# Windowed attention in patches of 8 rows by 16 columns, normalised after the value product

## The chip, the core and the metric

The kernel runs on one core of a Trainium2 chip. Its engines work side by side, each through its own instructions in order: PE (TensorE, matmuls and transposes into PSUM), DVE (VectorE), ACT (ScalarE), POOL (GpSimd, which here works on SBUF alone) and SP, which issues the DMAs. They wait for each other by semaphores. The metric is the device time of one execution in microseconds (us).

## What is computed

One encoder block over 1024 tokens (a grid of 16 rows by 64 columns) of width 1024. The normed input is projected into several branches; three give attention-like outputs that are gated, merged and added to the input, and a mixture of 16 experts follows. The change is in the first and third branch. In the windowed one, a query sees the 8 rows by 16 columns of keys around it, clipped to the grid:

```
r_start = clip(r - 4, 0, 8)          # 8 rows of keys
col_start = clip(col - 8, 0, 48)     # 16 columns of keys
scores = q . k_win + rpb[:, row_off, col_off]
probs = softmax(scores over the 8*16 keys)
out = probs . v_win                  # 6 heads of 64
```

The memory branch is plain attention of the 1024 tokens to 256 memory rows (4 heads of 64). The second branch is a recurrence whose result goes through a group norm.

## The kernel before

All products are fp32 or, where three terms are summed (high x high, low x high, high x low part), in fp32r. The stages in order: projections; the recurrence, with the remaining 35 projection jobs (`fill_gen`) put between its steps on PE; the attention stage; the three branch products with gating; the output product with the router; the experts.

In the attention stage `items` lists 48 windowed items and 16 memory items, which go through a software pipeline: at step n, `PIPE` gives each part of an item and its lag, and the order in which the parts are written is the order of instructions on every engine. A windowed item before is one row of 64 queries for a pair j of heads: the queries of the two heads lie in the two halves of the 128 stationary columns (`qb`, zero in the other head's 64 partitions), and the 512 keys are 8 whole rows. Columns outside the window get -1e30 from the bias table. The parts are `score` (L221 to L223 into PSUM tile `s`, then bias, maximum on DVE, L862), `exp` (L867, ACT), `recip` and `mul` (L870, L873, DVE: the probabilities are divided by their sum), `trans` (four transposes, L878, into PSUM tile `tr`, copied to `pt` by ACT, L880), `mix` (value product into PSUM tile `av`, L887, one half of the columns of PE for each head), `hi` and `lo` (L891, L894: the result is split into `yh` and `yl` for the branch products).

`na_load(j)` fetches and splits keys and queries, and transposes values (`VT`) in 15 blocks of 128 positions. `group_norm` is a generator with nine stops for each of six blocks of 512 tokens; from step `GN0` on, one stop is taken in each step. `NB_` gives the number of PSUM buffers of each tile name. A DMA waits in SP's order.

Of the kernel before, what the change touches and what calls it, by code (L numbers as in the profile page):

```python
# [35 lines left out]
S = 1024  # L36
D = 1024
NM = 256
# [25 lines left out]
def shape_constants():  # L64
# [16 lines left out]
    w, k = p % 64, np.arange(64)  # L81
    st = np.clip(w - 8, 0, 48)
    ok = (k[None] >= st[:, None]) & (k[None] < st[:, None] + 16)
    c["nmask"] = np.where(ok, 0.0, NEG)
# [22 lines left out]
def lay(inputs):  # L107
# [14 lines left out]
    pad = np.pad(a["na_rpb"][0], ((0, 0), (0, 0), (48, 48)))  # L122
    st = pad.strides
    toe = np.lib.stride_tricks.as_strided(pad[:, :, 63:], (6, 64, 15, 64), (st[0], -st[2], st[1], st[2]))
    o["rpb"] = np.ascontiguousarray(toe.reshape(3, 128, 15, 64).transpose(1, 0, 2, 3).reshape(128, 3, 960))
# [18 lines left out]
    return {k: np.ascontiguousarray(v) for k, v in o.items()}  # L144


@with_exitstack
def block_kernel(ctx: ExitStack, tc: tile.TileContext, T, out, dbg=None, upto=99):
# [36 lines left out]
    pna = scratch("pna", (9, 128, S))  # L185
# [41 lines left out]
    pps = pre_ctx.enter_context(tc.tile_pool(name="pps", bufs=1, space=PSUM, reuse_waits="tile"))  # L227
    pctx = ExitStack()
# [430 lines left out]
    def fill_gen():  # L659
        jobs = []  # L660
        for j0, j1, fn, sc_, dst in ((11, 14, AF.Copy, 0.125, pna[0:3]), (14, 20, AF.Copy, 1.0, pna[3:9]),
                                     (20, 22, AF.Copy, 0.125, pmq), (22, 46, AF.Tanh, 0.5, pgt)):
            jobs += [(j, fn, sc_, dst[j - j0]) for j in range(j0, j1)]
# [88 lines left out]
    def abank(tag):  # L752
        return aps.tile([128, 512], F32, name=tag, bufs=NB_[tag])

# [60 lines left out]
    na = {}  # L815

    def na_load(j):
        bias = ap.tile([128, 15, 64], F32, name="bias", bufs=2)
        q = ap.tile([128, S], F32, name="q", bufs=2)
        kt = ap.tile([128, S], F32, name="kt", bufs=1)  # L820
        VC = ap.tile([128, S], F32, name="VC", bufs=1)
        for t, src in ((kt, pna[3 + j]), (q, pna[j]), (VC, pna[6 + j]), (bias.rearrange("p r c -> p (r c)"), T["rpb"][:, j])):
            SP.dma_start(t, src)
        VT = ap.tile([128, 15, 128], F32, name="VT", bufs=2)
        qb = [ap.tile([128, 16, 2, 64], F32R, name=f"qb{v}", bufs=2) for v in "hl"]
        KT = [ap.tile([128, S], F32R, name=f"KT{v}", bufs=2) for v in "hl"]
        na[j] = bias, KT, qb, VT
        yield
        for v in (slice(0, 512), slice(512, 1024)):
            A.activation(KT[0][:, v], kt[:, v], AF.Copy)  # L830
            G.tensor_tensor(KT[1][:, v], kt[:, v], KT[0][:, v].bitcast(F32), op=OP.subtract)
            yield
        q = q.rearrange("p (r t) -> p r t", t=64)
        for h, r in ((0, 0), (1, 0), (0, 8), (1, 8)):
            hi, lo = (v[:, r:r + 8, h] for v in qb)
            V.tensor_scalar(hi, q[:, r:r + 8], C("hsel")[:, h:h + 1], None, op0=OP.mult)
            yield
            V.scalar_tensor_tensor(lo, q[:, r:r + 8], C("hsel")[:, h:h + 1], hi.bitcast(F32), op0=OP.mult, op1=OP.subtract)
            if r:
                yield  # L840
        G.tensor_tensor(bias, bias, C("nmask")[:, None, :].to_broadcast([128, 15, 64]), op=OP.add)
        for i0 in range(0, 15, 4):
            p = abank("tr")
            n = min(4, 15 - i0)
            for i in range(i0, i0 + n):
                t0 = i * 128 if i < 8 else (i - 8) * 128 + 64
                PE.transpose(p[:, (i - i0) * 128:(i - i0 + 1) * 128], VC[:, t0:t0 + 128], ident)
            A.activation(VT[:, i0:i0 + n], p[:, :n * 128].rearrange("p (i c) -> p i c", i=n), AF.Copy)
            yield

    def na_item(j, r):
        bias, KT, qb, VT = na[j]
        rs = min(max(r - 4, 0), 8)
        ro = rs - r + 7
        o = {}

        def score():
            s = abank("s")
            mm3(s, 0, 1, *(v[:, r].rearrange("p h t -> p (h t)") for v in qb), *(v[:, rs * 64:rs * 64 + 512] for v in KT))
            o["sb"] = sb = ap.tile([128, 512], F32, name="sb", bufs=4)  # L860
            o["st"] = st = ap.tile([128, 8], F32, name="st", bufs=4)
            V.tensor_tensor_reduce(out=sb, in0=s, in1=bias[:, ro:ro + 8, :].rearrange("p r c -> p (r c)"),  # L862
                                   scale=1.0, scalar=-3.0e38, op0=OP.add, op1=OP.max, accum_out=st[:, 0:1])
            V.tensor_scalar(st[:, 1:2], st[:, 0:1], -1.0, None, op0=OP.mult)

        def exp():
            A.activation(o["sb"], o["sb"], AF.Exp, bias=o["st"][:, 1:2], scale=1.0, accum_out=o["st"][:, 2:3])  # L867

        def recip():
            V.reciprocal(o["st"][:, 3:4], o["st"][:, 2:3])  # L870

        def mul():
            V.tensor_scalar(o["sb"], o["sb"], o["st"][:, 3:4], None, op0=OP.mult)  # L873

        def trans():
            p = abank("tr")
            for k in range(4):
                PE.transpose(p[:, k * 128:(k + 1) * 128], o["sb"][:, k * 128:(k + 1) * 128], ident)  # L878
            o["pt"] = ap.tile([128, 512], F32, name="pt", bufs=3)
            A.activation(o["pt"], p, AF.Copy)  # L880

        def mix():
            o["av"] = av = abank("av")
            for k in range(4):
                vi = (rs // 2 + k) if rs % 2 == 0 else 8 + (rs - 1) // 2 + k
                for h, q in enumerate((LO, UP)):
                    PE.matmul(av[q, 0:64], VT[:, vi, 64 * h:64 * h + 64], o["pt"][:, k * 128 + 64 * h:k * 128 + 64 * h + 64],  # L887
                              start=(k == 0), stop=(k == 3))

        def hi():  # L890
            A.activation(yh[:, j, r * 64:(r + 1) * 64], o["av"][:, 0:64], AF.Copy)  # L891

        def lo():
            V.tensor_sub(yl[:, j, r * 64:(r + 1) * 64], o["av"][:, 0:64], yh[:, j, r * 64:(r + 1) * 64].bitcast(F32))  # L894
# [3 lines left out]
    kv = ap.tile([128, 4, NM], F32, name="kv")  # L898
    kb = [ap.tile([128, 2, 2, NM], F32R, name=f"kb{v}") for v in "hl"]
    vm = ap.tile([128, 2, 256], F32, name="vm")  # L900
    qm = []

    def mem_load():
        SP.dma_start(kv, pkv.rearrange("j p t -> p j t"))
# [545 lines left out]
```

## Time and profile before

| | us |
|---|---|
| median of 3 runs (2363.93 to 2367.25) | 2364.92 |
| the profiled execution | 2365.14 |
| its span, first to last instruction | 2363.3 |
| PE busy in the span | 2251.8 (95%) |
| DVE busy | 1710.3 (72%) |
| ACT busy | 1338.9 (57%) |
| attention: first score to first branch product | 838.09 to 999.38 = 161.3 |

The execution lies 1.8 us above its span and 0.2 us above the median. PE's busy time counts each matmul to its modelled end, so neighbours overlap; what a stream of matmuls costs is read from the distance of their starts.

### The profile page before, as it was taken

What the parts mean: (1) busy time and instruction counts of PE and PEld (TensorE: products, weight loads), DVE (VectorE), ACT (ScalarE), POOL (GpSimd) and SP (SyncE); (2) the same over time, 40 slices, a digit from 0 to 9 for tenths busy, and PEclk for the clock granted to TensorE, in tenths of its full rate; (3) what the DMA queues carried; (4) which work ended last, traced back from release to release, by engine and by line L of the source; (5) the groups of instructions that cost most, each with busy time, mean ns of one, the idle gap of its engine ahead of it and who ended that gap; (6) DMA issues with size and microseconds to landing.
All of it is one profiled execution on the core that took longest, in us unless ns stands there. A gap on an engine that the chain in (4) does not pass through costs nothing.

```text
span 2363.3 us, 34407 instructions
## 1 busy us (share of the span) xinstructions
PE 2251.8 (95%) x12931; PEld 1825.8 (77%) x12931; DVE 1710.3 (72%) x2140; ACT 1338.9 (57%) x1631; POOL 602.7 (26%) x1187
## 2 busy tenths in 40 slices
PE   7999999999999989999938999999999999999996
PEld 6677787877778867777837888888888888888885
DVE  6556566556656278763276888888888988898887
ACT  5554233333333367721226777777777777777775
POOL 1000567666656334242040000000000000000001
PEclk9999999999999999999978999999999999999998
DMA  6335434443443252165396999999999999999995
GB/s 238 152 143 209 124 106 117 128 112 108 126 118 88 71 172 79 58 215 170 125 346 251 380 381 378 391 387 389 393 381 382 377 389 384 390 387 391 383 346 193
DMA packets 193911, 588.56 MB, mean 249 GB/s; under 512 B 53072, under 2 KB 97360, under 8 KB 144592
## 3 DMA queue, kind: packets, MB, share of 16 engines
q1 hardware_dynamic: 187120, 562.88, 64.6%
q0 software_dynamic: 4752, 17.30, 2.7%
q10 hardware_dynamic: 1872, 6.17, 0.7%
q8 instruction: 102, 1.67, 0.3%
q14 instruction: 65, 0.53, 0.1%
HBM read 517.56 MB, written 68.73 MB: 248 GB/s over the span
## 4 chain that ended last, share of the span: by engine, by line
PE 80%; DVE 11%; DMA 2%; POOL 2%; ACT 2%; issue 2%; SPq 0%; POOLq 0%; ACTq 0%; DVEq 0%
PE y L1317 14%; PE acc L695 12%; PE g L1305 5%; PE g L1306 5%; PE g L1308 5%; PE u L1305 5%; PE u L1306 5%; PE u L1308 5%; PE acc L221 3%; PE acc L222 3%; PE acc L223 3%; PE tr L1365 1%; DVE Gst L640 1%; PE av L887 1%; DVE rsl L218 1%
## 5 line engine op out<-in xcount | busy, mean ns | idle before, releaser
L1282 DVE TENSOR_TENSOR ewl<-raw,ewh 128x2048 fp32r<-128x2048 f32 x380 | 849.8, 2284 | 6.0 <-ACT ewh L1277 6.0
L1277 ACT ACTIVATE ewh<-raw 128x2048 fp32r<-128x2048 f32 x380 | 720.9, 1915 | 113.3 <-PE u L1306 84.4
L1324 POOL DMA_INDIRECT acc<-ye,idx x15 | 43.4, 2893 | 949.7 <-DVE ye L1323 872.2
L695 PE MATMUL acc<-hlo,wh 128*128 128x512 f32 x560 | 225.2, 402 | 0.0
L695 PE MATMUL acc<-hhi,wh 128*128 128x512 f32 x560 | 225.0, 402 | 0.0
L695 PE MATMUL acc<-hhi,wl 128*128 128x512 f32 x560 | 224.9, 402 | 0.0
L551 POOL TENSOR_TENSOR tmul<-tinv,blk 96x60 f32<-96x60 f32 (+24 forms) x496 | 174.3, 351 | 151.3 <-DMA blk<-ldr 113.7
L1305 PE MATMUL g<-ewh,xh 128*128 128x512 f32 x512 | 206.5, 403 | 0.0
L1305 PE MATMUL u<-ewh,xh 128*128 128x512 f32 x512 | 202.3, 395 | 0.0
L1306 PE MATMUL g<-ewh,xl 128*128 128x512 f32 x512 | 200.7, 392 | 0.0
L1306 PE MATMUL u<-ewh,xl 128*128 128x512 f32 x512 | 199.6, 390 | 0.0
L553 POOL TENSOR_TENSOR tinv<-tinv,tmul 96x60 f32<-96x60 f32 (+24 forms) x496 | 175.0, 353 | 38.9
L1317 PE MATMUL y<-ewh,ah 128*128 128x512 f32 x512 | 138.2, 392 | 0.7 <-ACT ah L217 0.7
L1317 PE MATMUL y<-ewl,ah 128*128 128x512 f32 x512 | 137.8, 391 | 0.0
L1317 PE MATMUL y<-ewh,al 128*128 128x512 f32 x512 | 137.7, 391 | 0.0
L1308 PE MATMUL g<-ewl,xh 128*128 128x512 f32 x512 | 137.4, 390 | 0.0
L1308 PE MATMUL u<-ewl,xh 128*128 128x512 f32 x512 | 137.1, 390 | 0.0
L218 DVE TENSOR_TENSOR wl<-wraw,wh 128x1024 fp32r<-128x1024 f32 (+1 forms) x60 | 76.0, 1268 | 66.0 <-ACT wh L217 66.0
L695 PEld LDWEIGHTS acc<-hlo,wh 128*128 128x128 f32 x560 | 106.0, 189 | 20.5
L695 PEld LDWEIGHTS acc<-hhi,wh 128*128 128x128 f32 x560 | 105.9, 189 | 20.1
L695 PEld LDWEIGHTS acc<-hhi,wl 128*128 128x128 f32 x560 | 105.9, 189 | 20.1
L217 ACT ACTIVATE ah<-tr 128x512 fp32r<-128x512 f32 x64 | 38.3, 598 | 143.6 <-PE tr L1365 143.6
(311 smaller groups left out, 4471.9 us busy)
## 6 DMA issues: line engine op xcount, KB each, us to landing
raw<-in_wg_dram SPq DMA_DIRECT2D x128, 1024.0 KB
raw<-in_wu_dram SPq DMA_DIRECT2D x128, 1024.0 KB
raw<-in_wd_dram SPq DMA_DIRECT2D x128, 1024.0 KB
wraw<-in_wt_dram SPq DMA_DIRECT2D x46, 512.0 KB
pt<-pz SPq DMA_DIRECT2D x16, 768.0 KB
pgt<-po SPq DMA_DIRECT2D x48, 256.0 KB
gt<-pgt SPq DMA_DIRECT2D x16, 768.0 KB
blk<-ldr SPq DMA_DIRECT2D x64, 96.0 KB
```

Source lines behind the costliest of these rows:

```text
L218: V.tensor_sub(lo, src, hi.bitcast(F32))
L221: PE.matmul(out_, lh, rh, start=(k_ == 0), stop=False)
L222: PE.matmul(out_, ll, rh, start=False, stop=False)
L551: G.tensor_tensor(tm[:, 0:m, 0:n], tt[:, 0:m, j:j + 1].to_broadcast([4 * NB, m, n]), lt[:, j, None, j + 1:32].to_broadcast([4 * NB, m, n]) ...
L553: G.tensor_tensor(tt[:, 0:m, j + 1:32], tt[:, 0:m, j + 1:32], tm[:, 0:m, 0:n], op=OP.add)
L695: PE.matmul(p, l[:, k], r[:, k, s0:s0 + 512], start=(k == 0 and i == 0), stop=(k == KD - 1 and i == 2))
L1277: A.activation(hi, raws[seq[n]], AF.Copy)
L1282: V.tensor_sub(lo, raws.pop(seq[n]), his[seq[n]].bitcast(F32))
L1305: PE.matmul(p, xh[:, 4 * b + k], wh[:, k], start=(b == 0 and k == 0), stop=False)
L1306: PE.matmul(p, xl[:, 4 * b + k], wh[:, k], start=False, stop=False)
L1308: PE.matmul(p, xh[:, 4 * b + k], wl[:, k], start=False, stop=(b == 1 and k == 3))
L1317: PE.matmul(py[n], l[:, 2 * b + k], r[:, k, n * 512:(n + 1) * 512], start=(f == 0 and b == 0 and i == 0 and k == 0), stop=(f == 3 and b == ...
```

## The change

A windowed item becomes a patch of 8 rows by 16 columns, 128 queries, for a pair of heads: 24 items in place of 48. Its keys are the 12 rows by 24 or 32 columns that hold every window of the patch, 288 or 384 keys for each head. Each head's score product uses only its 64 partitions of queries and keys, as a stationary of 64 rows, and the two heads write two banks of `s`. The bias table is laid out on the host for each kind of patch and carries the mask; it is fetched in six parts of 960 KB in place of three of 480 KB. The memory items get the same form. `mul` is gone: the value product runs on unnormalised probabilities, two more matmuls write the reciprocals, spread over 64 columns, beside it in `av`, ACT copies them to `rb`, and DVE multiplies (`out`). `yl` moves to POOL, half of the `pt` copies (all of the memory items') to DVE. `s` now takes four banks, so `gn` and `av` have one buffer each in place of two.

The projection jobs of the values store four overlapping column groups (`pvc`, 896 KB for a pair of heads in place of 512 KB), four copies and four DMAs for each half job in place of one; the keys of the first pair of heads are split straight from PSUM and never stored. The query split no longer masks. `group_norm` takes two stops in a step, from step 2 on.

```diff
@@ -51,11 +51,11 @@
-GN0 = 5
+GN0 = 2
...
-PIPE = (("hi", 6), ("exp", 1), ("recip", 2), ("lo", 6), ("mul", 2), ("score", 0), ("trans", 3), ("mix", 5))
-NB_ = dict(s=2, tr=2, gn=2, av=2)
+PIPE = (("out", 4), ("exp", 1), ("recip", 2), ("trans", 2), ("mix", 3), ("score", 0))
+NB_ = dict(s=2, tr=2, gn=1, av=1)
@@ -144,6 +137,26 @@
+NROW, NCOL, COL0S, CTYPE = 12, (24, 32, 24), (0, 8, 24, 40), (0, 1, 1, 2)
+BOFF = [0, 288, 672, 960]
+WSUM = sum(NCOL[t] for t in CTYPE)
@@ -679,6 +696,20 @@
                 _, fn, sc_, dst = jobs[n]
+                if n == 3:
+                    split_to(*(t[:, s0:s0 + 512] for t in kt0), p)
+                    continue
+                if 6 <= n < 9:
+                    at = 0
+                    for cg in range(4):
+                        w = NCOL[CTYPE[cg]]
+                        if cg % 2 == 0:
+                            po, a0 = pp.tile([128, 512], F32, name="po", bufs=2), 0
+                        A.activation(po[:, a0:a0 + 8 * w].rearrange("p (r c) -> p r c", c=w),
+                                     p.rearrange("p (r c) -> p r c", c=64)[:, :, COL0S[cg]:COL0S[cg] + w], AF.Copy)
+                        SP.dma_start(pvc[n - 6][:, at + s0 // 64 * w:at + (s0 // 64 + 8) * w], po[:, a0:a0 + 8 * w])
+                        at, a0 = at + 16 * w, 8 * w
+                    continue
@@ -750,7 +781,7 @@
     def abank(tag):
-        return aps.tile([128, 512], F32, name=tag, bufs=NB_[tag])
+        return aps.tile([128, 2, 512] if tag == "s" else [128, 512], F32, name=tag, bufs=NB_[tag])
@@ -812,173 +843,210 @@
+    def bias_load(m):
+        if m < 6:
+            bias[m] = ap.tile([128, 2, BOFF[3]], F32, name="bias", bufs=3)
+            SP.dma_start(bias[m], T["rpb"][m // 2, m % 2])
...
         def exp():
-            A.activation(o["sb"], o["sb"], AF.Exp, bias=o["st"][:, 1:2], scale=1.0, accum_out=o["st"][:, 2:3])
+            for h in range(2):
+                A.activation(o["sb"][h], o["e"][h], AF.Exp, bias=o["st"][:, 2 + h:3 + h], scale=1.0, accum_out=o["st"][:, 4 + h:5 + h])
...
-        def mul():
-            V.tensor_scalar(o["sb"], o["sb"], o["st"][:, 3:4], None, op0=OP.mult)
...
         def mix():
             o["av"] = av = abank("av")
-            for k in range(4):
-                vi = (rs // 2 + k) if rs % 2 == 0 else 8 + (rs - 1) // 2 + k
+            mix_of(o, av)
+            for h, q in enumerate((LO, UP)):
+                PE.matmul(av[q, 128:256], o["st"][:, 6 + h:7 + h].to_broadcast([128, 64]), ident, start=True, stop=True)
+            o["rb"] = rb = ap.tile([128, 128], F32, name="rb", bufs=2)
+            A.activation(rb, av[:, 128:256], AF.Copy)
+
+        def out():
+            y = ap.tile([128, 128], F32, name="y", bufs=3)
+            V.tensor_mul(y, o["av"][:, 0:128], o["rb"])
+            y = tokens(y)
+            A.activation(tokens(yh), y, AF.Copy)
+            G.tensor_tensor(tokens(yl), y, tokens(yh).bitcast(F32), op=OP.subtract)
...
+    def na_item(j, g):
+        rh, cg = g // 4, g % 4
...
+        def score(o):
+            KT, qb = na[j][:2]
+            s, st = abank("s"), o["st"]
+            for i, (a, b) in enumerate(((0, 0), (1, 0), (0, 1))):
                 for h, q in enumerate((LO, UP)):
...
+                    PE.matmul(s[:, h, :n], qb[a][q, rh, cg], grid(KT[b][q])[:, r0:r0 + NROW, c0:c0 + w], start=(i == 0), stop=(i == 2))
...
+            for h in range(2):
+                V.tensor_tensor_reduce(out=sb[:, h, :n], in0=s[:, h, :n], in1=bias[2 * j + rh][:, h, b0:b0 + n],
+                                       scale=1.0, scalar=-3.0e38, op0=OP.add, op1=OP.max, accum_out=st[:, h:h + 1])
+            V.tensor_scalar(st[:, 2:4], st[:, 0:2], -1.0, None, op0=OP.mult)
+
+        def trans(o):
+            o["pt"] = pt = ap.tile([128, 2, 384], F32, name="pt", bufs=3)
+            for h in range(2):
+                p = abank("tr")
+                for k in range(3):
+                    PE.transpose(p[:m, k * 128:(k + 1) * 128], o["sb"][h][:, k * m:(k + 1) * m], ident)
+                if h:
+                    V.tensor_copy(pt[:m, h], p[:m, :384])
+                else:
+                    A.activation(pt[:m, h], p[:m, :384], AF.Copy)
+
+        def mix(o, av):
+            for k in range(3):
+                for h, q in enumerate((LO, UP)):
+                    PE.matmul(av[q, 0:128], na[j][2][:m, cg, rh + k, 64 * h:64 * h + 64], o["pt"][:m, h, k * 128:(k + 1) * 128],
+                              start=(k == 0), stop=(k == 2))
...
     with tc.manual_schedule():
...
-        items = [(na_item, j, r) for j in range(3) for r in range(16)] + [(mem_item, j, i) for j in range(2) for i in range(8)]
-        side = {1: na_load(1), 17: na_load(2), 33: mem_load()}
+        items = [(na_item, j, g) for j in range(3) for g in range(8)] + [(mem_item, j, i) for j in range(2) for i in range(8)]
+        side = {0: na_load(1), 8: na_load(2), 16: mem_load()}
...
-            live.pop(n - 6, None)
+            live.pop(n - 4, None)
+            if n in (3, 7, 11):
+                bias_load(n // 4 + 3)
             extra = [g for g in extra if next(g, 0) is None]
             if n >= GN0:
+                next(gn, 0)
                 next(gn, 0)
```

On PE, in the steady part of the windowed items, one item stood before as follows (`s` scores, `tr` transposes, `av` the value product; a number behind x counts the same instruction in a row):

```order
L221 MATMUL s<-KTh,qbh 128x512
L222 MATMUL s<-KTh,qbl 128x512
L223 MATMUL s<-KTl,qbh 128x512
L878 MATMUL tr<-cst,sb 128x128 x4
L887 MATMUL av<-pt,VT 64x64 x8
```

Now one item, with a stop of the group norm behind its scores (`gn`), stands so:

```order
L963 MATMUL tr<-cst,sb 128x128 x6
L972 MATMUL av<-pt,VT 64x128 x6
L920 MATMUL av<-cst,st 64x128 x2
L950 MATMUL s<-KTh,qbh 128x288 x2
L950 MATMUL s<-KTh,qbl 128x288 x2
L950 MATMUL s<-KTl,qbh 128x288 x2
L816 MATMUL gn<-y_9140,cst 128x512
```

The transposes of the item two steps back and the value product of the one three steps back now stand between one item's scores and the next's. On DVE, in the same part, the order before was:

```order
L870 RECIPROCAL st<-st 128x1
L894 TENSOR_TENSOR yl<-av,yh 128x64
L873 TENSOR_SCALAR sb<-sb,st 128x512
L862 ISA sb,st<-s,bias 128x512
L862 ISA st 128x1
L864 TENSOR_SCALAR st<-st 128x1
```

Now it is (L926 is the multiplication that reads `av` and frees its one buffer; L965 the copy of the second head's transposes):

```order
L954 ISA sb,st<-s,bias 128x384
L954 ISA st 128x1
L954 ISA sb,st<-s,bias 128x384
L954 ISA st 128x1
L956 TENSOR_SCALAR st<-st 128x2
L833 TENSOR_TENSOR y_8858<-y_8858,gn 128x512
L926 TENSOR_TENSOR y<-av,rb 128x128
L911 RECIPROCAL st<-st 128x2
L965 COPY pt<-tr 96x384
```

The read of `av` stands behind the two bias passes of the item before, and behind the group norm's work (L833). On ACT, at the start of the stage, the order before was as follows (`KTh` the keys of the second pair of heads, `lg` the group norm's gate, which its tanh makes):

```order
L880 ACTIVATE pt<-tr 128x512
L891 ACTIVATE yh<-av 128x64
L867 ACTIVATE sb,st<-sb,st 128x512
L880 ACTIVATE pt<-tr 128x512
L780 ACTIVATE lg<-lg 128x1024
L891 ACTIVATE yh<-av 128x64
L867 ACTIVATE sb,st<-sb,st 128x512
```

Now it begins so (L908 the exponentials of an item's two heads):

```order
L908 ACTIVATE sb,st<-sb,st 128x384 x2
L967 ACTIVATE pt<-tr 96x384
L876 ACTIVATE KTh<-kt 128x512
L811 ACTIVATE lg<-lg 128x1024
L908 ACTIVATE sb,st<-sb,st 128x384 x2
```

The keys' first copy and `lg` now stand ahead of the third item's exponentials; before, `lg` stood behind the exponentials of six items of half the size.

## Rows read from the trace of the kernel before

**Rows 1.** Busy time by stretch: start and end, length, engines, PEclk, DMA, GB/s

```profile
core 0: us, PE busy (x) PEld busy (x) DVE busy (x) ACT busy (x) POOL busy (x), PEclk, DMA share, GB/s
...
838.10:858.00 19.90, 14.27 (x119) 9.41 (x117) 19.25 (x49) 11.99 (x30) 7.77 (x6) 1.00 0.63 221
858.00:955.00 97.00, 93.50 (x984) 71.63 (x984) 80.34 (x262) 74.90 (x194) 42.10 (x29) 0.98 0.24 82
955.00:991.60 36.60, 35.44 (x310) 25.61 (x308) 31.82 (x97) 30.18 (x99) 9.33 (x7) 1.00 0.09 30
```

**Rows 2.** Instructions in order of time on PE, one windowed item: start, length

```profile
933.67 0.50 PE L221 MATMUL s<-KTh,qbh 128*128 128x512 f32 x1
934.00 0.39 PE L222 MATMUL s<-KTh,qbl 128*128 128x512 f32 x1
934.24 0.39 PE L223 MATMUL s<-KTl,qbh 128*128 128x512 f32 x1
934.47 0.60 PE L878 MATMUL tr<-cst,sb 128*128 128x128 f32 x4
934.99 0.69 PE L887 MATMUL av<-pt,VT 128*64 128x64 f32 x16
935.61 0.50 PE L221 MATMUL s<-KTh,qbh 128*128 128x512 f32 x1
```

**Rows 3.** The same on PE, one memory item's value product

```profile
994.13 0.66 PE L963 MATMUL av<-pt,vm 128*64 128x128 f32 x8
994.73 0.65 PE L955 MATMUL tr<-cst,sb 128*128 128x128 f32 x4
```

**Rows 4.** The same on DVE: bias pass, its accumulator, negation, group norm

```profile
937.84 0.68 DVE L862 CUSTOM_DVE_ANT_0 sb<-s,bias 128x512 f32<-128x512 f32 x1
938.45 0.08 DVE L862 DVE_READ_ACCUMULATOR2_ANT st<- 128x1 f32 x1
938.56 0.15 DVE L864 TENSOR_SCALAR st<-st 128x1 f32<-128x1 f32 x1
938.63 0.68 DVE L802 TENSOR_TENSOR y<-y,gn 128x512 f32<-128x512 f32 x1
```

**Rows 5.** Groups of instructions, 838 to 1000: count, busy us, mean ns, idle before

```profile
L873 DVE TENSOR_SCALAR sb<-sb,st 128x512 f32<-128x512 f32 x48 | 35.9, 748 | 0.1
L867 ACT ACTIVATE sb<-sb,st 128x512 f32<-128x512 f32 x48 | 34.7, 723 | 17.0 <-DVE st L864 16.5 <-DVE st L870 0.4
...
L941 ACT ACTIVATE sb<-s,st 128x256 f32<-128x256 f32 x32 | 14.9, 474 | 4.0 <-DVE st L936 3.8
...
L935 DVE TENSOR_REDUCE st<-s 128x2 f32<-128x512 f32 x16 | 10.9, 682 | 0.0
...
L805 POOL TENSOR_TENSOR y<-y,b 128x512 f32<-128x512 f32 x6 | 8.1, 1345 | 33.8 <-ACT yh L891 26.9 <-ACT y L804 6.9
...
L970 DVE TENSOR_TENSOR yl<-av,yh 128x128 fp32r<-128x128 f32 x16 | 4.6, 285 | 3.1 <-ACT yh L967 2.9
...
L786 ACT ACTIVATE y<-gn 128x512 f32<-128x512 f32 x6 | 3.6, 599 | 2.0 <-PE gn L785 2.0
L787 ACT ACTIVATE b<-gn 128x512 f32<-128x512 f32 x6 | 3.6, 595 | 0.0
```

**Rows 6.** The start of the stage: SP's issue, POOL's wait, traffic

```profile
839.68 0.44 SPq L759 DMA_DIRECT2D lg<-plat  x1
...
847.75 1.28 POOL L777 TENSOR_TENSOR y<-y,y 128x512 f32<-128x512 f32 x1 [0.94 <-DMA y<-yrw]
...
844.00:846.00 2.00, 1.32 (x8) 0.81 (x7) 1.93 (x6) 1.71 (x5) 1.10 (x2) 1.00 1.00 328
```

**Rows 7.** A stall on the second pair's keys, and PE's granted clock behind it

```profile
885.83 0.63 ACT L830 ACTIVATE KTh<-kt 128x512 fp32r<-128x512 f32 x1 [2.43 <-DMA kt<-pna]
...
888.23 1.09 PE L878 MATMUL tr<-cst,sb 128*128 128x128 f32 x4 [1.77 <-DVE sb L873]
...
889.00:890.00 1.00, 1.00 (x16) 0.75 (x16) 1.00 (x3) 1.00 (x3) 1.00 (x2) 0.50 0.10 39
```

More of the change, by code (lines that the diff above doesn't have):

```diff
@@ L144, in lay, with window_bias @@
     return {k: np.ascontiguousarray(v) for k, v in o.items()}
+NROW, NCOL, COL0S, CTYPE = 12, (24, 32, 24), (0, 8, 24, 40), (0, 1, 1, 2)
+BOFF = [0, 288, 672, 960]
+WSUM = sum(NCOL[t] for t in CTYPE)
+def window_bias(rpb, rh, ct):
+    cg = (0, 1, 3)[ct]
+    r, c = 8 * rh + np.arange(8), 16 * cg + np.arange(16)
+    kr, kc = 4 * rh + np.arange(NROW), COL0S[cg] + np.arange(NCOL[ct])
+    r0, c0 = np.clip(r - 4, 0, 8), np.clip(c - 8, 0, 48)
+    rows, cols = (kr[None] >= r0[:, None]) & (kr[None] < r0[:, None] + 8), (kc[None] >= c0[:, None]) & (kc[None] < c0[:, None] + 16)
+    inside = rows[:, None, :, None] & cols[None, :, None, :]
+    ir = np.clip(kr[None] - r[:, None] + 7, 0, 14)
+    ic = np.clip(kc[None] - c[:, None] + 15, 0, 30)
+    t = rpb[:, ir[:, None, :, None], ic[None, :, None, :]]
+    out = np.full(t.shape, NEG, np.float32)
+    out[:, inside] = t[:, inside]
+    return out.reshape(3, 2, 128, -1).transpose(0, 2, 1, 3)
 @with_exitstack
@@ new lines, in na_load @@
+        VC = ap.tile([128, 16 * WSUM], F32, name="VC", bufs=1)
+        qb = [ap.tile([128, 2, 4, 128], F32R, name=f"qb{v}", bufs=2) for v in "hl"]
+        KT = kt0 if j == 0 else [(ap if j == 1 else nq).tile([128, S], F32R, name=f"KT{v}") for v in "hl"]
+        na[j] = [KT, qb]
+        for rh in range(2):
+            SP.dma_start(q[:, 512 * rh:512 * rh + 512], pna[j][:, 512 * rh:512 * rh + 512])
+            if j == 0 and rh == 0:
+                bias_load(0)
+        if j:
+            kt = ap.tile([128, S], F32, name="kt", bufs=1)
+            SP.dma_start(kt, pna[3 + j])
@@ L851, in na_item @@
[L851 to L854, printed above, removed]
+        for rh in range(2):
+            hi, lo = (v[:, rh].rearrange("p g (r c) -> p g r c", c=16) for v in qb)
+            src = q[:, 512 * rh:512 * rh + 512].rearrange("p (r g c) -> p g r c", r=8, g=4)
+            A.activation(hi, src, AF.Copy)
+            (G if j else V).tensor_tensor(lo, src, hi.bitcast(F32), op=OP.subtract)
+            yield
+        VT = ap.tile([128, 4, 4, 128], F32, name="VT", bufs=2)
@@ new lines, in na_load, with attention @@
+        na[j].append(VT)
+        for cg in range(4):
+            p = abank("tr")
+            w = NCOL[CTYPE[cg]]
+            for i in range(4):
+                PE.transpose(p[:4 * w, i * 128:(i + 1) * 128], VW[cg][:, 4 * i * w:4 * (i + 1) * w], ident)
+            src, dst = p[:4 * w].rearrange("p (i c) -> p i c", i=4), VT[:4 * w, cg]
+            if cg % 2:
+                V.tensor_copy(dst, src)
+                yield
+            else:
+                A.activation(dst, src, AF.Copy)
+    def attention(score_of, trans_of, mix_of, tokens):
@@ L896, in na_item @@
-        return locals()
[L898 to L901, printed above, removed]
+            mix_of(o, av)
[3 more added lines that the diff above has]
+            A.activation(rb, av[:, 128:256], AF.Copy)
@@ L939, in exp, with tokens @@
-        def exp():
-            for h in range(2):
-                A.activation(o["sb"][:, h], o["s"][:, h * 256:(h + 1) * 256], AF.Exp, bias=o["st"][:, 2 + h:3 + h], scale=1.0,
-                             accum_out=o["st"][:, 4 + h:5 + h])
-        def recip():
-            V.reciprocal(o["st"][:, 6:8], o["st"][:, 4:6])
-        def mul():
-            for h in range(2):
-                V.tensor_scalar(o["sb"][:, h], o["sb"][:, h], o["st"][:, 6 + h:7 + h], None, op0=OP.mult)
-        def trans():
+        def tokens(y):
+            return y if y.ndim == 2 else y[:, 6 + j, ts]
@@ new lines, in score @@
+        def score(o):
+            s, st = abank("s"), o["st"]
+            for i_, (a, b) in enumerate(((0, 0), (1, 0), (0, 1))):
+                for h, q in enumerate((LO, UP)):
+                    PE.matmul(s[:, h, :NM], qm[j][a][q, ts], kb[b][q, j], start=(i_ == 0), stop=(i_ == 2))
+            V.tensor_reduce(st[:, 0:2], s[:, :, :NM], axis=AX.X, op=OP.max)
+            V.tensor_scalar(st[:, 2:4], st[:, 0:2], -1.0, None, op0=OP.mult)
+            sb = ap.tile([128, 2, 384], F32, name="sb", bufs=4)
+            o["e"], o["sb"] = ([t[:, h, :NM] for h in range(2)] for t in (s, sb))
```

162 lines of the change are left out of this document (69 added, 93 removed).

## Prediction

> **What bounds the kernel now.** The change touches the attention stage, so I read the busy time by stretch there first [rows 1]. From 858 to 955 PE is busy 93.5 of 97.0 us while DVE has 80.3: PE is the bound. In the first 20 us it is DVE, 19.25 of 19.90, with PE at 14.27. From 955 on the memory items run, PE again in front (35.4 of 36.6). Then I read one windowed item on PE in order of time [rows 2]: 1.94 us from one score to the next, 0.80 for three score products (starts some 0.24 apart), 0.52 for four transposes, 0.62 for the value product. Its sixteen records are eight pairs, the heads side by side: 0.46 at 0.058 a pair, with 0.16 left. 48 × 1.94 = 93 us and 36.6 for the memory items [rows 1]; the remaining 32 of the 161.3 us (table above) are the slow start, the group norm and the two ends. So the stage is bound by throughput: queues are deep enough that PE seldom waits.
>
> **The change, part by part.**
>
> *Work.* DVE loses the normalisation, 48 × 748 ns = 35.9 us [rows 5], and PE's score products have two thirds of the columns, for twice the queries. If throughput stayed the limit, this would be a large gain. But there is only one `av` buffer, and the order on PE and DVE shown above ties them into one ring for each item: PE's value product (L972) waits until DVE's L926 has read the item before; L926 stands on DVE behind the two bias passes, which need the scores that PE issued last; and the next scores stand on PE behind that value product. No other work of either engine shortens the ring; the transposes lie under DVE's part. So I price an item by the ring:
>
> - From the last score's start to DVE: a score runs 0.39 with 0.235 to the next start [rows 2], so 0.16 of drain, with a hand-over about 0.25.
> - Bias passes: 0.61 from start to start for 512 columns [rows 4]; between L970 (285 ns at 128 columns, [rows 5]) and L802 (0.68 at 512, [rows 4]) a column costs 1.03 ns, so a mean of 336 columns (half the patches have 288, half 384) takes 0.43. Each has an accumulator read of 0.11, and the negation 0.07 follows: 2 × 0.54 + 0.07 = 1.15.
> - L926, 128 columns from PSUM: 0.29 as L970, with hand-over 0.34.
> - Value product and reciprocals: 12 + 4 records, eight pairs of 128 columns at 0.11 (twice 0.058), and 0.16 for the change of form: 1.03. The memory product of before agrees, four pairs in 0.60 [rows 3].
> - Scores: 336/512 × 0.235 = 0.154 each. If the two heads' products, on the two halves of PE's rows, run together: 3 × 0.154 = 0.46; if one after the other, 0.92. No row has products on half the rows. The nearest is the value product, whose two halves of the columns do run together [rows 2], so I take 0.46 and keep 0.92 as a rival.
>
> Sum 3.2 us, × 24 = 77. [...]
>
> *Memory items.* The same ring with one reduction (682 ns, [rows 5]) in place of the two passes: 0.25 + 0.78 + 0.34 + six pairs 0.82 + scores of 256 columns 0.35 = 2.5, × 16 = 40 (before 36).
>
> ACT has two exponentials (474 ns at 256, 723 at 512 columns, [rows 5], so about 0.55 each), a copy of 0.45, and two small passes of 0.3: 2.2 an item, below 3.2, and it is off the ring. POOL has `yl`, 0.3 to 0.6, likewise covered. If that cover went, 2.2 would not bind until the ring fell below it.
>
> *Group norm.* Two stops in a step, with one `gn` buffer. Its twelve multiplications on DVE (0.61 each, L802, [rows 4]) stand inside the ring: 7.3 us. In three of the six blocks the centring product and the statistics fall into one step; PE then waits until ACT has copied and squared the first from the one buffer, 2 × 0.60 [rows 5], with the product of 0.24 to 0.6, ACT's own queue and two hand-overs about 2.4: 7. In the other three, POOL's addition (1345 ns, [rows 5]) and the multiplication behind it share a step, about 0.6 each on DVE: 2. Together 17. Before, PE was the bound and DVE's share was hidden. From below: only the 7.3, if ACT is early; from above: 25, if all six blocks wait 2.4.
>
> *Start.* Before the first score may start, `VC` (896 KB) and a bias part come ahead: 1.5 us. Then ACT's copy of the second pair's keys and the tanh of `lg` stand ahead of the third item's exponentials, and the group norm starts three steps earlier. Traffic is full there, 328 GB/s [rows 6]; before, POOL's first addition, behind 5760 KB, could start at 847.75 [rows 6]. By the diff 7936 KB now come ahead, 2176 KB or 6.6 us more, so near 854. On PE the first centring product, which needs it, stands behind the fourth item's scores, three periods of 3.2 after a first score at 839.5, so about 849, and everything on PE waits behind it: some 5, and 1 for ACT's waits ahead of it. I take 6, from 0 (if the later pieces come in another order than I count) to 9.
>
> *Rest.* Value copies and key splits of the later pairs fall on DVE, four 512-column copies: 3. Splits of weights stand behind the last group-norm stop, inside memory items, four at 0.7: 3. Value jobs have 18 more copies and DMAs in the stage before, which PE bounds: 1. The pipeline is shorter, fill less by about 5, but the drain at the end is bound by the ring's latency, more by as much: 0. `mul` (L873) and `lo` vanish from DVE's queue, counted by the ring already.
>
> Sum: 77 + 40 + 17 + 1.5 + 6 + 3 + 3 + 1 = 148.5 against 161.3: 13 less. The stages behind are the same instructions and are taken to shift. The profiled execution took 2365.14 (0.2 above the median): 2352 for it, **2351** for a median.
>
> **The rivals.**
>
> *B. The two heads' scores run one after the other.* Ring 3.66 and 2.85: 24 × 0.46 + 16 × 0.35 = 16.6 more, 2368: no change. For it: no row shows it otherwise, and all score products before use the whole array; against it the column halves of rows 2.
>
> [...]
>
> *D. The group norm and the start cost little.* ACT, at 2.2 of 3.2, copies and squares while DVE is in its part of the ring, and data are in time: 9 for the group norm's waits and 6 for the start go, 2337.
>
> **How the numbers follow.** Main case 0.45 (2343 to 2359), D 0.2 (2333 to 2343), B 0.18 (2359 to 2372), C 0.09 (above 2372); a start or group norm far worse than priced, 0.08, lands with B. A measurement of this kernel tells about 0.2%, 4.7 us. Faster: all of main and D and a little of B, 0.68; same: most of B and of the last case, 0.18; slower: C and the rest, 0.14. Range 2334 to 2371: below lies an eighth of D and all where the ring is shorter than priced; above C.
>
> **What would show it.** The trace should have a windowed item every 3.2 us (3.8 with a group-norm multiplication) and a memory item every 2.5; PE's idle time before L972 ended by DVE's L926 (`y`), nearly 1 us each; the two halves of L950 starting within 0.05 of each other (0.15 apart is B); PE waiting before the group norm's products between 845 and 855; the granted clock 1.00 in most stretches; and the first branch product near 986 in place of 999.4. It is wrong if the ring is not what PE waits for, or if the stage's DVE parts differ from their 512-column rows.

## The result and the profile after

The changed kernel took 2383.45 us in the median of four runs (2381.43 to 2384.89), the kernel before beside it 2365.09: a ratio of 1.0076, 95% interval 1.0059 to 1.0093. It is slower by 18 us; the prediction had 2351 and at most 2371. The profiled execution took 2382.75, its span 2380.9, 17.6 longer than before. The first score stands at 842.80 in place of 838.09 and the first branch product at 1018.6 in place of 999.38, and from there to the end it is 1362.3 against 1363.9: all of the loss is in the attention stage.

The busy time of the changed kernel by stretch, columns as in [rows 1]:

```profile
838.10:858.00 19.90, 13.72 (x80) 9.53 (x82) 8.47 (x29) 9.38 (x24) 6.17 (x6) 0.67 0.99 369
858.00:955.00 97.00, 76.47 (x658) 55.63 (x654) 50.96 (x172) 56.81 (x169) 47.59 (x49) 0.91 0.30 102
955.00:1018.60 63.60, 47.08 (x442) 33.57 (x441) 38.00 (x101) 34.43 (x125) 21.30 (x31) 0.92 0.18 57
```

No engine is full any more. PE falls from 93.5 to 76.5 of 97 us, though part of that runs at the lower clock, DVE from 80.3 to 51.0. DVE's work did go, and the stage became a chain of waits. One plain item on PE in order of time (start, length, engine, and the idle time before with its releaser) has what [rows 2] showed before:

```profile
885.29 0.52 PE L950 MATMUL s<-KTl,qbh 64*128 64x384 f32 x2
885.74 0.86 PE L963 MATMUL tr<-cst,sb 128*96 128x128 f32 x6
887.36 0.88 PE L972 MATMUL av<-pt,VT 96*64 96x128 f32 x12 [0.76 <-DVE y L926]
888.07 0.39 PE L920 MATMUL av<-cst,st 128*64 128x128 f32 x4
888.39 0.44 PE L950 MATMUL s<-KTh,qbh 64*128 64x384 f32 x2
888.67 0.34 PE L950 MATMUL s<-KTh,qbl 64*128 64x384 f32 x2
888.85 0.34 PE L950 MATMUL s<-KTl,qbh 64*128 64x384 f32 x2
889.12 0.66 PE L832 MATMUL gn<-cst,grb 128*128 128x128 f32 x4
```

The wait of 0.76 for L926 is the forecast ring; before the value products it comes in 22 of the 40 items, 20.7 us in all. The value product and the reciprocals take 1.03 to the next score (1.03 forecast). The two heads' products of 384 columns (x2) take 0.34 together and the next pair starts 0.18 later, while a single product of 512 columns on all rows had 0.24 to the next start [rows 2], from which 0.18 is the estimate for 384. So the halves of PE's rows do run side by side here: rival B is out.

The waits of PE and of DVE from 838 to 1020, with total, number and longest, tell where the rest went:

```profile
PE av L972 <- DVE y L926: 13.8, 12, 2.5
PE av L1035 <- DVE y L926: 6.9, 10, 1.2
PE gn L816 <- POOL y L808: 6.1, 4, 4.3
PE gn L838 <- DVE y L833: 4.1, 3, 2.1
PE gn L822 <- ACT b L818: 3.5, 3, 1.2
PE gn L832 <- ACT grb L828: 2.6, 3, 1.1
...
DVE rinv_t L210 <- PE gn L822: 6.4, 3, 2.2
DVE y L926 <- ACT rb L922: 6.2, 4, 3.2
...
DVE y L840 <- POOL y L836: 4.3, 3, 1.6
```

PE waits at all four kinds of the group norm's products (L816, L822, L832, L838), each in three or four of the six blocks, 16.3 us in all. DVE waits for the group norm and ACT as well, 16.9 us in the three lines shown, at or ahead of the read (L926) on which PE's next value product waits.

Another thing that the forecast did not have is in the groups of the same stretch (count, busy us, mean ns):

```profile
L972 PE MATMUL av<-pt,VT 96*64 96x128 f32 x144 | 11.8, 306 | 4.7 <-DVE y L926 4.3 <-DVE st L911 0.4
...
L956 DVE TENSOR_SCALAR st<-st 128x2 f32<-128x2 f32 x24 | 11.2, 466 | 0.8
L926 DVE TENSOR_TENSOR y<-av,rb 128x128 f32<-128x128 f32 x39 | 11.0, 283 | 4.8 <-ACT rb L922 4.8
L954 DVE CUSTOM_DVE_ANT_0 sb<-s,bias 128x288 f32<-128x288 f32 x24 | 10.0, 455 | 14.3 <-PE s L950 14.3
...
L1020 DVE TENSOR_SCALAR st<-st 128x2 f32<-128x2 f32 x16 | 5.0, 313 | 0.5
```

L956 negates two numbers a partition and takes 466 ns in the mean, 0.17 at least. In order of time it stands like this at 890, with POOL's work beside it:

```profile
889.98 1.26 POOL L877 TENSOR_TENSOR KTl<-kt,KTh 128x512 fp32r<-128x512 f32 x1 [1.80 <-ACT KTh L876]
...
890.31 0.96 DVE L956 TENSOR_SCALAR st<-st 128x2 f32<-128x2 f32 x1
891.18 0.68 DVE L833 TENSOR_TENSOR y<-y,gn 128x512 f32<-128x512 f32 x1
891.78 0.28 DVE L926 TENSOR_TENSOR y<-av,rb 128x128 f32<-128x128 f32 x1
...
891.91 0.70 PE L838 MATMUL gn<-lg,g 128*128 128x512 f32 x1 [2.14 <-DVE y L833]
```

It begins under POOL's L877 and ends with it: 890.31 + 0.96 = 891.27 against 889.98 + 1.26 = 891.24. In 12 of the 24 windowed items its end falls within 0.06 us of that of a POOL instruction; in the other twelve no POOL instruction is under way when it starts, and it takes 0.17. Before, the windowed items' negation was of one column, 0.15 [rows 4].

### The profile page after: what moved, and what is told of

Read it like the earlier page. It is cut to its first block, busy times and chain, and to the rows that moved or that the text cites. A ratio compares the mean times of both kernels' runs of the same rounds, so it can differ in the third digit from the quotient of the medians.

```text
span 2380.9 us, 33660 instructions
## 1 busy us (share of the span) xinstructions
PE 2235.4 (94%) x12614; PEld 1810.2 (76%) x12614; DVE 1666.4 (70%) x2012; ACT 1317.6 (55%) x1622; POOL 615.4 (26%) x1227
## 4 chain that ended last, share of the span: by engine, by line
PE 72%; DVE 9%; POOL 8%; issue 3%; DMA 3%; ACT 2%; SPq 2%; POOLq 0%; DVEq 0%; ACTq 0%
PE y L1389 14%; PE acc L726 8%; PE g L1377 5%; PE g L1378 5%; PE g L1380 5%; PE u L1377 5%; PE u L1378 5%; PE u L1380 5%; PE acc L235 3%; POOL tmul L568 3%; PE acc L237 3%; PE acc L236 3%; POOL tinv L570 3%; PE tr L1437 1%; SPq L575 1%
## 5 line engine op out<-in xcount | busy, mean ns | idle before, releaser
L1354 DVE TENSOR_TENSOR ewl<-raw,ewh 128x2048 fp32r<-128x2048 f32 x380 | 849.7, 2284 | 6.5 <-ACT ewh L1349 6.5
```

What stands on the lines that cost most here:

```text
L1354: V.tensor_sub(lo, raws.pop(seq[n]), his[seq[n]].bitcast(F32))
```

## The experiments

Three theories were open. **Ring:** the one value bank with the order on DVE sets the pace, and its price was too low. **Pace:** two stops of the group norm in a step put dependent instructions side by side in in-order queues. **Clock:** the pauses lower PE's clock (rival C). Smaller suspects were the start and the negation's wait beside POOL (L956, 9.7 us in the trace of the changed kernel), which the expectations call the port. Differences below are between a kernel's median and that of the kernel before in the same comparison; the changed kernel stands at +18.4. Each ratio has an interval of some 3.5 us either way, so a difference of less than about 5 us between two versions is not shown by their times alone.

**The group norm out of the loop**: its stops then run behind the last item.

```diff
-GN0 = 2
+GN0 = 100
```

> All of the group norm runs behind the last item; the work is the same. Theory that the group norm inside the loop costs some 35 us (17 were forecast): windowed items come every 3.2 to 3.6 us, the last memory item's scores stand near 965 in place of 1012, and the group norm alone then takes about 50 us, so that the whole is near 2385. Rival (the clock and POOL's port make the items slow by themselves): windowed items stay near 4 us or above, and the last scores come after 985.

2442.66, +76 (ratio 1.0318, 1.0296 to 1.0340). Loop and remainder by stretch:

```profile
843.90:968.00 124.10, 94.76 (x1007) 70.03 (x1008) 79.74 (x269) 75.51 (x267) 32.97 (x50) 1.00 0.26 94
968.00:1074.00 106.00, 47.72 (x154) 24.29 (x150) 12.66 (x29) 24.29 (x49) 42.91 (x36) 0.54 0.19 65
```

The loop, from first to last score, takes 124.8 us against 170.0 in the changed kernel: the group norm costs 45 us in it. What PE did in that time is read from four stretches: the loop of the changed kernel, the group norm's products alone in it, the loop without them, and the group norm's products in the stage before (the first number behind the length is PE's busy time).

```profile
842.80:1013.10 170.30, 129.64 (x1114) 93.22 (x1114) 93.78 (x291) 97.13 (x305) 73.70 (x81) 0.89 0.30 105
842.80:1013.10 170.30, 26.15 (x96) 12.60 (x96) 9.17 (x18) 6.51 (x12) 0.89 0.30 105
843.89:968.95 125.06, 95.72 (x1018) 70.68 (x1018) 79.88 (x269) 76.42 (x271) 33.32 (x50) 1.00 0.26 93
838.09:999.38 161.29, 23.41 (x96) 11.95 (x96) 9.19 (x18) 6.52 (x12) 0.99 0.25 84
```

PE's own products of the group norm take 26.2 us, the same 1018 other products 103.5 in place of 95.7, at a granted clock of 0.89 in place of 1.00, and PE is idle for 40.7 in place of 29.3: 26.2 + 7.8 + 11.3 is the 45. More than half is thus work of PE, which was there before too (23.4), when PE was the bound.

The eight plain windowed items come every 3.04 us (288 columns) and 3.37 (384), memory items every 2.62, where 3.2 in the mean and 2.5 were forecast. Over all 24 windowed items it is 3.49, since 13 of them, beside the splits and value transposes of the data fetched next, take 3.95 to 4.24. With the 6 us forecast for such copies and splits the ring's price was right: 77 + 40 + 6 = 123 against 124.8. And the clock is 1.00 through the whole loop, with PE's pauses at every item (busy 94.8 of 124.1 us), so the ring's pauses did not lower it: rival C is out. Where it is lower, PE also waited for the group norm: 0.91 from 858 to 955 in the changed kernel, with 8.9 us of such waits, the longest 2.1, and 0.54 here behind the loop, with PE busy 47.7 of 106 us. The remainder was a miss: 105 us to the first branch product in place of 50, as six blocks in sequence at the lower clock hide under nothing.

**The old kernel at the new pace**, which is this part of the change alone, two stops in a step and the start at step 2 in place of 5:

```diff
-GN0 = 5
+GN0 = 2
...
                 next(gn, 0)
+                next(gn, 0)
```

> The kernel before with the changed kernel's pace of the group norm alone: two stops in a step, from step 2. Theory that the pace makes PE and DVE wait whatever the items are: 6 to 14 us slower than before, 2371 to 2379. Rival (with two banks and deeper queues the old items absorb it; the pace costs only beside a ring): within 3 us of 2365.

2390.47, +24.3 (1.0107, 1.0090 to 1.0123), more than the theory asked. Its stretch of 97 us, and its waits:

```profile
858.00:955.00 97.00, 80.31 (x690) 58.53 (x689) 62.12 (x177) 55.56 (x136) 43.90 (x31) 0.88 0.26 90
```

```profile
PE gn L785 <- POOL y L777: 16.2, 6, 5.3
PE gn L791 <- ACT b L787: 3.5, 3, 1.2
...
DVE yl L894 <- ACT yh L891: 17.5, 19, 3.7
DVE rinv_t L196 <- PE gn L791: 11.5, 6, 3.8
```

With two banks each and no ring, the old items too lose PE from 93.5 to 80.3 and clock from 0.98 to 0.88. From first score to first branch product PE is idle 26.0 us in place of 11.4, and busy 160.7 in place of 149.9. The waits of PE shown were not there before, and the reciprocal's was 0.6; DVE's wait for L891 was 15.1 and is hardly new. So the pace makes such waits without any ring. The longest of them (5.3 us, at 849.7) falls at the earlier start, which was not tried apart from the two stops.

**The ring's bank.** First the one bank was halved between two items:

```diff
-            o["av"] = av = abank("av")
+            o["av"] = av = avs[len(avn) % 2]
+            avn.append(0)
```

> The one av bank is split into two halves that items take in turn; nothing else is changed. Ring theory (the value product waits for the read of the item before, which stands behind the bias passes): that wait goes, the next bound is the chain scores, bias passes, exponential, transposes, product over two steps, about 2.5 us for a windowed item without group norm (3.4 now) and about 2.1 for a memory item (2.62 now); the time falls by 10 to 18 us, to 2365 to 2373. Rival (the group norm's products and waits on PE and the clock set the pace, the ring only fills their gaps): memory items shorten, windowed ones hardly; the gain is under 8 us.

2385.51, +19.0. Memory items kept 2.62 and the value product kept its wait for DVE's read of the item before (7.0 us in six waits from 900 to 960, 6.3 in six in the changed kernel): here the wait goes by the tile, not by its half. So this tells nothing of the ring. Then the banks were dealt anew, one pair for the scores, and the freed ones to the value product, to the group norm, or to both:

```diff
-NB_ = dict(s=2, tr=2, gn=1, av=1)
+NB_ = dict(s=1, tr=2, gn=1, av=2)
...
+NB_ = dict(s=1, tr=2, gn=2, av=1)
...
+NB_ = dict(s=1, tr=2, gn=2, av=2)
```

> Banks alone: one pair of score banks in place of two, two for the value product in place of one, the group norm keeps its one. Ring theory (the value product waits for the read of the item before, which stands behind the bias passes): this wait goes; a windowed item without group norm comes every 2.5 to 2.7 us in place of 3.0 to 3.4, and the stage is 10 to 20 us shorter, 2363 to 2373. The scores then wait for the bias passes of the item before, under which transposes and value product lie; memory items, whose exponentials read the score banks, stay near 2.6. Rival (the group norm's products on PE set the pace): under 6 us.

> Banks alone: one pair of score banks, two for the group norm, one for the value product. Theory that the group norm's one bank is a large part of its 45 us: PE's waits for DVE's multiplication before the gate product (2.1 us each) go and the next block's centring does not wait for the last; 10 us or more less, 2373 or below. Rival (its waits are for results, copies, squares and reciprocals, not for the bank): under 5 us, since items without group norm keep their 3.0 to 3.4.

> Banks alone: one pair of score banks, two each for transposes, group norm and value product. Ring theory: the gains of the two runs before add up, some 20 to 28 us less, 2355 to 2363, below the kernel before. Rival (both only move the wait to the bias passes or the exponentials): not below 2370.

2384.57 (+16.7), 2386.11 (+18.3) and 2378.25 (+10.4, 1.0042). With two value banks the plainest windowed items came every 2.4 to 2.55 us, as expected, so the wait was the ring. But few items are plain. PE then waited 10.6 us for POOL's addition in place of 6.1, and memory items rose from 2.62 to 3.06 behind the exponentials that read `s`. With two banks for the group norm alone PE's wait for the gate's multiplication (L838, 4.1 us) was gone and the time was not shorter. The gains in time fell short of the theory in all three, and each stayed within its rival's bound. All three also halve the score banks, so no bank was tried quite by itself.

**The order of the parts, the value bank single**:

```diff
-PIPE = (("out", 4), ("exp", 1), ("recip", 2), ("trans", 2), ("mix", 3), ("score", 0))
+PIPE = (("trans", 3), ("mix", 4), ("exp", 1), ("recip", 2), ("out", 4), ("score", 0))
...
-            o["st"] = ap.tile([128, 8], F32, name="st", bufs=4)
+            o["st"] = ap.tile([128, 8], F32, name="st", bufs=5)
```

> The order of the parts alone (transposes and product one step later, the read of the value bank ahead of the item's bias passes; one more small buffer for the sums). Banks as in the changed kernel. Ring theory: with one value bank too the ring goes; plain windowed items every 2.3 to 2.6, memory items 2.0 to 2.2; with the group norm's waits as they are, 10 to 18 us less, 2365 to 2373. Rival (the one bank, not the order, makes the ring): 3.0 to 3.4 and 2.6 as now, within 3 of 2383.

2377.45, +11.3 (1.0044). Plain windowed items come every 2.42 (288 columns) and 2.55 (384), plain memory items every 1.94, with the one bank: order and bank together make the ring, and either undoes it. The time fell by 7 us only, less than forecast: items with a group-norm product still take 3.3 to 10.8 us, the first 14.2. PE's waits for POOL's addition rose from 6.1 to 18.3 us. Half of that, 9.2, is at the first block, whose data come no sooner for faster items: its product starts at 857.4, in the changed kernel at 854.4.

**The stops apart, the negation, the start.** One stop is put behind the transposes and one behind the scores; the negation is made of one column twice; the first loads are ordered anew:

```diff
+                if part == "trans" and n >= GN0:
+                    next(gn, 0)
...
                 next(gn, 0)
-                next(gn, 0)
...
-            V.tensor_scalar(st[:, 2:4], st[:, 0:2], -1.0, None, op0=OP.mult)
+            for h in range(2):
+                V.tensor_scalar(st[:, 2 + h:3 + h], st[:, h:h + 1], -1.0, None, op0=OP.mult)
...
-            if j == 0 and rh == 0:
-                bias_load(0)
...
         SP.dma_start(VC, pvc[j])
+        if j == 0:
+            bias_load(0)
...
-        for m in (1, 2):
-            bias_load(m)
+        bias_load(1)
+        gn = group_norm()
+        next(gn)
+        bias_load(2)
```

> The two stops of the group norm in a step are taken apart: one behind the transposes, one behind the scores; nothing else. Theory that most of its 45 us are waits, since a stop's product stands on PE, or its reciprocal on DVE, right behind the stop on whose result it waits: value product and scores now lie between, so that the waits for copy and square (1.2), for the gate's multiplication (2.1) and part of those of the reciprocal (2.2) shrink; 8 to 15 us less, 2368 to 2375. Rival (it costs by its work, not by its place): within 3 of 2383.

> The negation of two columns becomes two negations of one column, in both kinds of item; nothing else. Theory that the two-column form waits for POOL's instruction under way (12 of 24 ended with one; mean 466 ns against 168 at least, 9.7 us over all items, all of it in the ring): the single ones run at 0.15 each and the time falls by 6 to 9 us, to 2374 to 2377. Rival (what ends there would only be waited for elsewhere in the ring, or the wait belongs to the place and not to the form): under 2 us.

> Order of the first loads alone: the values of the first pair ahead of the bias parts, and the group norm's first loads ahead of the second pair's. Theory that the start is set by SP's order (values landed 3.4 us late behind 960 KB of bias; the group norm's loads stood behind a load that waits for the one value buffer): first score at 840 or before in place of 842.8, PE's wait for POOL's addition of 4.3 us gone; 5 to 9 us less, 2375 to 2379. Rival (traffic is full whatever the order, and some other piece is then late): under 3 us.

The stops apart: 2376.16, +10.0 (1.0039). PE's wait for copy and square fell from 3.5 to 0.7 and that for the gate's multiplication (4.1) went, while that for POOL's addition rose from 6.1 to 10.3. So some 8 us in the time belonged to the place of the two stops side by side.

The negation: 2379.80, +13.3 (1.0049), some 5 us less than the changed kernel, a little under the forecast and at the edge of what the times resolve. In the trace it is plain: the windowed items' single-column form takes 151 ns in the mean of 48 and 154 at most, with none that waits:

```profile
L957 DVE TENSOR_SCALAR st<-st 128x1 f32<-128x1 f32 x48 | 6.5, 151 | 0.0
```

So the wait belongs to the form: 466 ns in the mean on two columns, 151 on one. Two columns alone do not make the wait: the reciprocal on two columns (L911) took 166 ns at most in 40 of the changed kernel, 13 of them beside a POOL instruction.

The start: 2390.63, +24.1, a miss by its sign. The first score did come at 840.56. But the second pair's keys were now behind the group norm's loads, and ACT, in order, waited 9.5 us for them with everything else queued behind:

```profile
854.72 0.63 ACT L876 ACTIVATE KTh<-kt 128x512 fp32r<-128x512 f32 x1 [9.53 <-DMA kt<-pna]
```

**A later start of the group norm.**

```diff
-GN0 = 2
+GN0 = 8
```

> The group norm starts at step 8 in place of 2; nothing else. Theory that the wait of 9.6 us at the fourth item is for data that come late: it goes, and with it 5 to 7 us, less what the last blocks cost among the memory items (2 to 3 us more): 2377 to 2381. Rival (the same stops cost the same anywhere): 2383 within 2.

2389.78, +21.9 (1.0087), a miss too: the loads are issued by the first stop, one step ahead of the product that needs them, so the wait moves with it, to 8.06 us ahead of the product at 881.7. They were issued from 869.9 on, right behind the third pair's queries, keys and values (1920 KB), and the traffic was 378 to 431 GB/s from 870 to 882. So this start met another rush of loads, and what a late start costs with free traffic was not tried.

**All at once**: order, stops apart, negation, and a milder order of the loads (values ahead of the bias as above, the next pair's values two steps later).

```diff
         if j:
             yield
             yield
+            SP.dma_start(VC, pvc[j])
```

> Both of those, with the single-column negations and the values of the first pair loaded ahead of the bias parts, those of a later pair two steps later. If the ring, the places of the stops, the port and the start are the causes, their gains add: 25 to 40 us less than the changed kernel, 2343 to 2358, faster than the kernel before. If they hide each other's waits: 2360 or above.

2365.51, -0.7 (0.9994, 0.9984 to 1.0003), short of the range. The gains add to 19 us, about what three of them gave singly (7, 8 and 5). PE still waits 18.6 us for POOL's addition, 9.9 of it once, at 853.9, for the first block's data, and 8.7 in four later blocks.

**The pace spread**: one stop a step from step 0, a second in every fourth.

```diff
-GN0 = 2
+GN0 = 0
...
                 next(gn, 0)
-                next(gn, 0)
+                if n % 4 == 3:
+                    next(gn, 0)
```

> The changed kernel with the group norm's stops spread over the whole loop (one in each step, a second one in every fourth, from step 0) and nothing else. Theory that the pace of two stops in a step is most of the loss, as in the old kernel, which lost 24 us by it alone: 14 to 24 us less than the changed kernel, 2359 to 2369. Rival (the ring leaves no gap in which the group norm could hide, whatever its pace): 2375 or above.

> That pace and the new order of the parts alone. Theory: the ring's 10 us and the pace's 15 to 20 add, 2350 to 2362; the negation and the start account for the rest up to the run with all four (5 to 10 us). Rival (they hide each other): no better than with the pace alone.

> That pace (the second stop apart from the first) with the new order of the parts, the single-column negations and the order of the first loads. If the pace, the ring, the port and the start are the causes: 2338 to 2355, faster than the kernel before by 10 us or more. If the group norm's waits do not go with the pace: 2360 or above.

The pace alone: 2378.89, +12.4 (1.0050), some 6 us and not 14 or more, so that the time is the rival's. The last score came 15 us earlier (997.8 for 1012.8), but the last block was left behind the last item's scores:

```profile
998.01 1.12 PE L816 MATMUL gn<-y,cst 128*128 128x512 f32 x2
1000.31 1.05 PE L822 MATMUL gn<-cst,b 128*128 128x2 f32 x8 [1.18 <-ACT b L818]
...
1008.66 1.12 PE L838 MATMUL gn<-lg,g 128*128 128x512 f32 x2 [0.78 <-DVE y L833]
1014.71 0.79 PE L235 MATMUL acc<-yh,wh 128*128 128x512 f32 x1 [4.92 <-ACT wh L231]
```

From last score to first branch product it is 16.9 us where the changed kernel has 5.8: 11 of the 15 were given back. With the new order: 2358.14, -8.4 (0.9969, 0.9958 to 0.9981). With all four: 2353.04, -13.5 (0.9948, 0.9937 to 0.9960). In these two later runs the second stop stands apart from the first, behind the transposes. Order, pace and stops apart gave 7, 6 and 8 us singly, 21 in all, and 27 together. It may be that an item without the ring has slack in which a stop can wait, and that with one stop a step there is one wait in it; the 6 us between 21 and 27 are too few to show it.

**The ends.** The loads stay at step 0, the other stops begin at step 4, a second one stands in every third step.

```diff
-                if part == "trans" and n % 4 == 3:
+                if part == "trans" and n >= 4 and n % 3 == 1:
                     next(gn, 0)
...
-            if n >= GN0:
+            if n == 0 or n >= 4:
                 next(gn, 0)
```

> The version with all four edits, with the group norm's loads issued at step 0 as there, but its other stops from step 4 on, and a second stop in every third step, so that none is left behind the loop. If what is left of its loss is PE's wait of 11.4 us for POOL's first addition and the 13 us between the last scores and the first branch product: both shrink, 4 to 9 us less than the 2353 measured there, 2344 to 2349. Rival (the denser pace gives back what the ends gain): 2353 within 3.

2348.30, -17.7 (0.9925, 0.9912 to 0.9939): a version faster than both kernels. Its stretches:

```profile
838.10:858.00 19.90, 13.91 (x101) 9.83 (x101) 9.65 (x44) 11.28 (x34) 7.40 (x7) 0.83 0.98 377
858.00:955.00 97.00, 88.19 (x894) 66.17 (x892) 63.88 (x254) 72.11 (x234) 54.44 (x63) 1.00 0.31 108
955.00:983.00 28.00, 21.14 (x187) 14.47 (x184) 16.78 (x48) 17.02 (x54) 13.58 (x17) 0.93 0.27 95
```

PE is back at 88 of 97 us, the clock at 1.00, and the first branch product stands at 980.8.

## Why the prediction was wrong

The forecast stage was 148.5 us from 838.1 on; it took 180.5. Of the 32 us between, 22 lie in the group norm with its start (45 against 17 + 6) and 3 in the first score (4.7 us behind 838.1 against 1.5). The rest is in the items and the end: 124.8 from first to last score without the group norm and 5.8 behind the last, against 123.

- *The ring:* right in mechanism and price. Forecast 3.2 and 2.5, measured 3.04 to 3.37 in plain windowed items, 3.49 over all 24, and 2.62 without the group norm. The wait of PE for L926, the halves side by side, and the idle of ACT came as said.
- *The group norm:* this step failed. It was priced at 17, with another 6 for the start; measured, the loop is 45 longer with it. The working counted DVE's multiplications and one wait in each block: PE's for the square in three, POOL's addition in the other three. PE's own products of the group norm, 23.4 us in the kernel before, were put at nothing but one of 0.24 to 0.6 within a wait, without a reason why the ring's pauses should hold the rest. The runs showed 26.2 us of these products, 7.8 more for PE's other products at the lower clock and 11.3 more of idle PE. All four kinds of product wait, in three or four blocks each, and the reciprocal on DVE; part of these 16.3 us of PE's waits replaces pauses that the ring has anyway. An item with a group-norm product took 3.6 to 7.9 us (the first 9.6), where 3.8 was forecast. Worse, the price was set as an addition to the change, from rows in which the old pace is hidden, while the pace was an edit of its own: in the old kernel it costs 24 us.
- *The negation beside POOL:* missing from the forecast. On two columns it waits for POOL's instruction: 9.7 us of excess over its shortest in the trace (7.2 windowed, 2.5 memory), 5 us in the time when undone, at the edge of the noise.
- *Start:* first score forecast 839.5, came at 842.8. PE waited 3.4 us for values that shared the traffic with two bias parts, 369 GB/s at a DMA share of 0.99 from 838 to 858. The 4.3 us for POOL's addition were near the 5 priced for it.
- *Clock, rival C:* wrong as a rival. Its chance of 0.09 rested on the author's estimate that PE's pauses in the ring lower the clock, as it stood lower behind the stall of [rows 7]. No run shows that of the ring: the loop without the group norm ran at 1.00. The lower clock came with the group norm's waits, 0.91 from 858 to 955; there a value product took up to 1.9 us to the next score in place of 1.03. In PE's busy time it is 7.8 us on the items' products and 2.7 on the group norm's (26.15 against 23.41 before), but no run tried it by itself.
- *Rivals B and D:* out. The chance of a slower kernel was 0.14, most of it for the clock; the case that came (the group norm far worse) had 0.08 and was placed with B, up to 2372.

What stays open: PE's account says what PE did in the 45 us, not what would have to change to save them. No run kept the group norm's waits and raised the clock, or took out DVE's own work for it (9.2 us) alone, so no single cause has a share. That order, pace and stops apart do more together (27) than singly (21) is not shown.

## What to carry to other kernels

Work interleaved by stops must be priced on every engine that it uses, and by the distance between dependent stops: here PE's own products were the largest part (26.2 of 45 us), and two stops side by side made an in-order engine wait for the neighbour (some 8 us in the time). The edit of a pace is tested alone first, on the kernel before: it cost 24 us there, without any ring. Where a single bank turns a pipeline into a ring, restore the slack (order of the parts, one step more of lag) together with the pace; the two, with the stops apart, made the 8 us gain over the kernel before, and a later choice of the stops' steps with the smaller edits 18. And removed busy time, 36 us of DVE here, is no forecast of time where the next bound is a wait.

## What the hardware showed beyond that

DVE's TENSOR_SCALAR on two columns took up to 1.3 us beside POOL, 0.17 without, and 0.15 on one column; its RECIPROCAL on two columns never took over 0.17 in 40 of the changed kernel. The granted clock stayed at 1.00 in a loop in which PE was idle at every item (busy 94.8 of 124.1 us), and was 0.54 where one block of group norm followed the other (47.7 of 106 us busy). Two products of 384 columns on the two halves of PE's rows had 0.18 us to the next pair's start, which is also the estimate for one of 384 columns on all rows from the 0.24 of 512 columns [rows 2].
